# GpSimd's sums read their two operands 24 bytes apart modulo 32

## The chip, the core and the metric

The kernel runs on one core of one Trainium2 chip. A time is device microseconds of one execution, from the host's side of the device; the span is what the profiler shows between the first and the last instruction of one profiled execution. Every run computes the same layer stack on the same input.

## What is computed

Two layers of a decoder trunk on a sequence of 512 tokens and 1024 channels, in float32. Cut to what matters here:

```python
for l in range(DEPTH):                                   # DEPTH = 2
    x = x + 0.5 * swiglu(rms_norm(x, ffn1_norm[l]), gate1[l], up1[l], down1[l])   # D_FF = 2816
    h = rms_norm(x, mix_norm[l])
    a, g, q, k, v = split(h @ w_in[l])
    conv_out = silu(rms_norm(causal_depthwise_conv(a * sigmoid(g), conv_w[l]) + conv_b[l]))  # width 31
    diff_out = differential_attention(q, k, v, ...)
    x = x + concat([conv_out, diff_out]) @ w_out[l]
    x = x + 0.5 * swiglu(rms_norm(x, ffn2_norm[l]), gate2[l], up2[l], down2[l])
```

where `swiglu(h, g, u, d) = (silu(h @ g) * (h @ u)) @ d`. There are four feed-forward parts (two per layer) and two mixers.

## The kernel before

**Split weights.** A float32 matrix product is made of three products of rounded parts. Each weight tile arrives by DMA in a buffer `wraw` (128 partitions x 1024 columns, a ring of five). ScalarE rounds it into `whi` (L101, L364), VectorE or GpSimd subtracts the rounded part and writes the rest into `wlo` (L102, L368). TensorE then multiplies hi x hi, hi x lo and lo x hi. `chunk` loads such a tile for the plain products and the mixer; `by_halves` and `gather` are variants for single places.

**Units.** Each feed-forward part first does five blocks of hidden features in the plain way, and the other 17 in *units*. A unit makes a two by two block product from seven smaller ones instead of eight (Strassen's scheme in Winograd's form). For this it needs sums of weight blocks as well as the blocks: GpSimd makes them, four per unit, in `Unit.sums` (L355 to L358): `d` from a gate and an up block, `u1 + u2` in place, then `m0` and `m1`, each made from the one before. There are 17 gate and up units (`GateUp`) and 8 down units (`Down`) in each feed-forward part, 100 in all. One unit keeps TensorE busy for some 10 us. A unit's raw weights lie in three buffers of the `wraw` ring, called A (`u`), B (`g`) and C (`more`, for `m0` and `m1`), and one buffer of 512 columns, D (`d`), of which there is only one. So the first sum of a unit's load waits for VectorE's `lo("D")` of the unit before.

**Order.** `Unit.body` writes out the order of a unit: it loads the next unit, goes through its own seven products, and between them calls the next unit's `hi` and `lo` for A, B, D, C, and what is left of the previous ones (`rest`, `finish`, `combine`). A tile scheduler places the instructions on each engine; every engine then works strictly in its own order. ScalarE also moves finished products out of PSUM (`keep`, L396, L413, L433); the next product into that bank waits for it. `combine` (L685 to L692) makes sums of hidden features, `hold` and `hs`, which the down units read; after the last gate and up unit of a group it is called at once (`soon`).

**The mixer.** GpSimd makes all 31 taps of one of four channel groups of the convolution and 10 taps of another: ScalarE multiplies a shifted `u` by a tap (L971, `prod`), GpSimd adds it to `yp` (L972). Squares of the result are summed in `csum` (L953), and `conv_finish` multiplies the result by a row factor (L998) and subtracts rounded parts (L1003). The convolution's input tile `u` has PAD = 30 columns of zeros in front, so its data starts 120 bytes into the tile. VectorE makes the other taps (L986), reading the same `u` at every shift. All tiles of the mixer and the units start at multiples of 32 bytes in a partition. The part `wlo` of the chunks for queries, keys, values and the output projection is made by GpSimd (L102), raw minus hi.

**Space.** `ones_r` is made wider by `SPACE` unused columns, which sets where later tiles lie.

Of the kernel before, what the change touches and what calls it, by code (L numbers as in the profile page):

```python
# [11 lines left out]
F32 = mybir.dt.float32  # L12
F32R = mybir.dt.float32r
I32 = mybir.dt.int32
AF = mybir.ActivationFunctionType
ALU = mybir.AluOpType
AX = mybir.AxisListType

P = 128
DEPTH = 2  # L20
SEQ = 512
# [8 lines left out]
TAPS = 31  # L30
# [15 lines left out]
PLAIN = PARTS[0][1]  # L46
PIN = False

SPACE = 392

POOL_TAPS = (TAPS, 0, 0, 10)

# [16 lines left out]
def trunk(ctx: ExitStack, tc: tile.TileContext, xt, par, lamv, relb, onehot,  # L69
          gu1, dn1, wag, wqkv, wout, gu2, dn2, out):  # L70
    nc = tc.nc
    V, S, G, T = nc.vector, nc.scalar, nc.gpsimd, nc.tensor

    const = ctx.enter_context(tc.tile_pool(name="const", bufs=1))
    small = ctx.enter_context(tc.tile_pool(name="small", bufs=2))
    act = ctx.enter_context(tc.tile_pool(name="act", bufs=1))
    wp = ctx.enter_context(tc.tile_pool(name="wp", bufs=1))
    tmp = ctx.enter_context(tc.tile_pool(name="tmp", bufs=2))
# [3 lines left out]
    def f32(ap):  # L82
        return ap.bitcast(F32)
# [7 lines left out]
    RING = {"wraw": 5, "whi": 4, "wlo": 4, "wraw2": 1, "whi2": 2, "wlo2": 2}  # L91

    def ring(tag, n=1024):
        dt = F32 if "raw" in tag else F32R
        return wp.tile([P, n], dt, tag=tag, name=tag, bufs=RING[tag])

# [7 lines left out]
            tc.keep_in_program_order(low)  # L104

    def chunk(src, eng=None, pin=False):
        raw, hi, lo = ring("wraw"), ring("whi"), ring("wlo")
        nc.sync.dma_start(raw, src)
        parts_of(raw, hi, lo, eng, pin=pin)
        return hi, lo  # L110

    def by_halves(src):

        raw, got = ring("wraw"), []
        nc.sync.dma_start(raw, src)
        for h in (slice(0, 512), slice(512, 1024)):
            got.append((ring("whi2", 512), ring("wlo2", 512)))
            parts_of(raw[:, h], *got[-1])
        return got
# [35 lines left out]

    ones_r = const.tile([P, P + SPACE], F32R, tag="ones_r", name="ones_r")[:, :P]
    V.memset(f32(ones_r), 1.0)
# [8 lines left out]
    for k0, k1 in ((0, 1), (1, 4), (4, KT)):  # L166
        h = slice(k0 * P, k1 * P)
# [14 lines left out]
    def col(l, name, i=0):  # L182
        c = _AT[name] + i
        return pars[l][:, c : c + 1]
# [149 lines left out]
    def pinned(ins, pin=PIN):  # L334
        if pin:
            tc.keep_in_program_order(ins)
        return ins
# [4 lines left out]
    def by_two(t):  # L342
        return t.rearrange("p (n c) -> p n c", n=2)

    class Unit:
# [3 lines left out]

        def __init__(self, fp):  # L350
            self.fp = fp
            self.parts, self.raw, self.cols = {}, {}, {}

        def sums(self, u1, u2, g1, g2, d, m0, m1):
            G.tensor_tensor(d, g1, u1, op=ALU.add)  # L355
            G.tensor_tensor(u1, u1, u2, op=ALU.add)  # L356
            G.tensor_tensor(m0, u1, g1, op=ALU.add)  # L357
            G.tensor_tensor(m1, m0, g2, op=ALU.add)  # L358

        def hi(self, k, pin=PIN):  # L360
            tag, n = self.WIDE[k]
            hi, lo = ring("whi" + tag, n), ring("wlo" + tag, n)
            self.parts[k] = hi, lo
            pinned(S.activation(hi[:, : self.cols[k]], self.raw[k][:, : self.cols[k]], AF.Copy), pin)  # L364

        def lo(self, k, pin=PIN):
            (hi, lo), c = self.parts[k], self.cols[k]
            pinned(V.tensor_tensor(out=lo[:, :c], in0=self.raw[k][:, :c], in1=f32(hi[:, :c]), op=ALU.subtract), pin)  # L368

        def w(self, k, b):  # L370
            c = slice(b * P, (b + 1) * P)
# [83 lines left out]
    class GateUp(Unit):  # L455
# [5 lines left out]
            self.soon = n == 2 * gated.pairs - 1 and n + 1 == gated.many  # L461

        def load(self):
            u, g = ring("wraw"), ring("wraw")
            nc.sync.dma_start(u, self.src[1])
            nc.sync.dma_start(g, self.src[0])
            d, more = ring("wraw2", 512), ring("wraw")
            h = slice(0, 512), slice(512, 1024)
            self.sums(u[:, h[0]], u[:, h[1]], g[:, h[0]], g[:, h[1]], d, more[:, h[0]], more[:, h[1]])
            self.raw = {"A": u, "B": g, "C": more, "D": d}  # L470
            self.cols = {k: n for k, (_, n) in self.WIDE.items()}

        AT = {"u2u1": ("A", 0), "u2": ("A", 4), "g1": ("B", 0), "g2": ("B", 4), "g1u2u1": ("C", 0), "all": ("C", 4),
              "g1u1": ("D", 0)}
# [28 lines left out]
    class Down(Unit):  # L503
# [7 lines left out]
        def load(self):  # L511
            A, B = 2 * self.q, 2 * self.q + 1
            whole, over, J = min(self.many, 8), max(self.many - 8, 0), self.steps * P

            def pull(raw, at, m, k, end):
                while k < end:
                    half, f = divmod(self.m0 + k, HALF)
                    b, w = m * HALF + f, 1
                    while (b + w) % 8 and k + w < end and f + w < HALF:
                        w += 1  # L520
                    c = b % 8
                    nc.sync.dma_start(raw[:, at : at + w * P], self.dn[half, b // 8][:, c * P : (c + w) * P])
                    at, k = at + w * P, k + w

            u, g, d = ring("wraw"), ring("wraw"), ring("wraw2", 512)
            pull(u, 0, B, 0, whole)
            pull(g, 0, A, 0, whole)
            more = ring("wraw")
            at = {"D": J, "C": 2 * J}
            raw = {"D": d, "C": more}  # L530
            where = ("D", "D") if J + 2 * over * P <= 512 else ("D", "C")
            self.ninth = []
            for n, m in enumerate((A, B)):
                k = where[n]
                self.ninth.append((k, at[k] // P))
                pull(raw[k], at[k], m, whole, self.many)
                at[k] += over * P

            def odd_even(t):
                t = t[:, : 2 * J].rearrange("p (j e c) -> p e j c", e=2, c=P)  # L540
                return t[:, 0], t[:, 1]

            def row(t, n):
                return t[:, n * J : (n + 1) * J].rearrange("p (j c) -> p j c", c=P)

            self.sums(*odd_even(u), *odd_even(g), row(d, 0), row(more, 0), row(more, 1))
            self.raw = {"A": u, "B": g, "C": more, "D": d}
            self.cols = {"A": whole * P, "B": whole * P, **at}

        def weights(self, wt, j):  # L550
            k, b = {"u2u1": ("A", 2 * j), "u2": ("A", 2 * j + 1), "g1": ("B", 2 * j), "g2": ("B", 2 * j + 1),
# [287 lines left out]
    def mixer(l, pr, after, turn):  # L839
        with tc.tile_pool(name="mix", bufs=1) as mp, tc.tile_pool(name="mt", bufs=2) as mt:  # L840
# [104 lines left out]
            csum = mp.tile([P, SEQ], F32, tag="csum", name="csum")  # L945

            def conv_square(c, y):
                if c == 0:
                    S.activation(csum, y, AF.Square)
                else:  # L950
                    sq = mt.tile([P, SEQ], F32, tag="csq", name="csq", bufs=1)
                    S.activation(sq, y, AF.Square)
                    G.tensor_tensor(csum, csum, sq, op=ALU.add)  # L953

                if c == CT - 1:
                    for k in range(CT):
                        tc.keep_in_program_order(
                            G.tensor_scalar(ys[k], ys[k], ghalf[l][:, k : k + 1], None, op0=ALU.mult)
                        )

            def conv_taps(c, n, then=None):

                wc = _AT["conv_w"] + c * TAPS
                yp = None
                if n:
                    yp = mp.tile([P, SEQ], F32, tag="yp%d" % (n < TAPS), name="yp")
                    G.tensor_scalar(yp, us[c][:, 0:SEQ], pars[l][:, wc : wc + 1], col(l, "conv_b", c),
                                    op0=ALU.mult, op1=ALU.add)
                    for t in range(1, n):
                        p = mt.tile([P, SEQ], F32, tag="prod", name="prod")  # L970
                        S.activation(p, us[c][:, t : t + SEQ], AF.Copy, scale=pars[l][:, wc + t : wc + t + 1])  # L971
                        G.tensor_tensor(yp, yp, p, op=ALU.add)  # L972
                if n == TAPS:
                    ys[c] = yp
                    conv_square(c, yp)
                    return
                y = bank("y", "ps_y")
                if not n:
                    V.tensor_scalar(y, us[c][:, 0:SEQ], pars[l][:, wc : wc + 1], col(l, "conv_b", c),
                                    op0=ALU.mult, op1=ALU.add)  # L980
                else:
                    V.tensor_scalar(y, us[c][:, n : n + SEQ], pars[l][:, wc + n : wc + n + 1], None, op0=ALU.mult)

                ys[c] = us[c][:, PAD:]
                for t in range(n + 1 if n else 1, TAPS):
                    V.scalar_tensor_tensor(ys[c] if t == PAD and not n else y, us[c][:, t : t + SEQ],  # L986
                                           pars[l][:, wc + t : wc + t + 1], y, op0=ALU.mult, op1=ALU.add)
                if then is not None:
                    then()
                if n:  # L990
                    V.tensor_tensor(ys[c], y, yp, op=ALU.add)
                conv_square(c, ys[c])
# [137 lines left out]
            for half, t in ((0, slice(0, SEQ)), (1, slice(SEQ // 2, SEQ)), (1, slice(0, SEQ // 2))):  # L1130
                if t.stop == SEQ:
                    w = [None] * 4 if half else wo
                for m in range(KT):
# [3 lines left out]
                    for kk in range(4):  # L1137
                        k = half * 4 + kk
# [108 lines left out]
```

## Time and profile before

| | |
|---|---|
| median of 3 runs | 1775.47 us (1773.9 to 1775.86) |
| the profiled execution | 1775.77 us |
| its span | 1774.0 us |
| granted TensorE clock | 0.999 |
| TensorE busy | 99% of the span |
| VectorE, GpSimd, ScalarE busy | 80%, 56%, 56% |
| DMA | 177.89 MB, mean 100 GB/s |

Busy shares say which engine is full over the whole span; TensorE is. A row of a group gives the line, the engine, output and inputs, the count, then the busy time in us and the mean duration in ns, then the engine's idle time ahead of those instructions and what ended it. A row of the waits reads: who waited, for whom, us in total, times, the longest. A row of the timeline or of the chain starts with the start in us from the span's beginning and the duration in us. Durations of TensorE's matmuls overlap, so its pace is read from the distance of starts.

### The profile page before, as it was taken

The page shows a single profiled execution, that of the slowest core. Times are in us where ns is not written, and L with a number is a line of the kernel's source. Part 1 is how long each engine was busy: PE and PEld are TensorE (multiplying, and loading weights), DVE is VectorE, ACT ScalarE, POOL GpSimd, SP SyncE. Part 2 cuts the span into 40 slices and gives each one's busy share as a digit, 9 for nine tenths or more (in the row PEclk, how much of TensorE's full clock was granted, in tenths as well). Part 3 has the DMA queues.
Part 4 walks back from the last instruction along what each step waited for, and adds up shares of the span by engine and source line. Part 5 has one row for each costly group of instructions (what it writes and reads, how often), then busy time and mean ns, then how long its engine had stood idle before and what let it go on. Part 6 is the DMA issues. An engine that isn't in the chain of part 4 may idle for free.

```text
span 1774.0 us, 30565 instructions
## 1 busy us (share of the span) xinstructions
PE 1762.0 (99%) x11869; PEld 1624.0 (92%) x11869; DVE 1418.2 (80%) x2021; ACT 996.4 (56%) x1591; POOL 999.9 (56%) x665
## 2 busy tenths in 40 slices
PE   9999999999999999999999999999999999999999
PEld 7899999988788899999988999999887888999998
DVE  6978878868857978888778788887788588788785
ACT  6456566545844456556534665665558354565663
POOL 3176666369863156766403666653798532567661
PEclk9999999999999999999999999999999999999999
DMA  6232333332122223323332333324231232333332
GB/s 225 91 117 98 108 108 105 124 106 96 36 84 84 84 96 108 108 96 114 112 108 71 103 101 108 108 94 157 71 110 34 72 108 71 108 96 108 108 105 75
DMA packets 74226, 177.89 MB, mean 100 GB/s; under 512 B 8951, under 2 KB 30726, under 8 KB 74080
## 3 DMA queue, kind: packets, MB, share of 16 engines
q1 hardware_dynamic: 72480, 174.10, 29.9%
q8 instruction: 93, 1.52, 0.4%
q0 software_dynamic: 1312, 1.67, 0.3%
q14 instruction: 53, 0.43, 0.1%
q10 hardware_dynamic: 288, 0.16, 0.0%
HBM read 173.79 MB, written 3.42 MB: 100 GB/s over the span
## 4 chain that ended last, share of the span: by engine, by line
PE 84%; DVE 9%; issue 3%; POOL 2%; ACT 1%; DMA 1%; SPq 0%; DVEq 0%; ACTq 0%
PE ps_pair L378 44%; PE ps_pair L142 5%; PE ps_pair L141 5%; PE ps_pair L138 5%; DVE wlo L368 4%; PE ps_d L141 2%; PE ps_d L138 2%; PE ps_d L142 2%; PE ps_sc L1018 2%; PE ps_d L378 2%; PE ps_pair L894 2%; PE ps_pair L896 2%; PE ps_pair L895 2%; PE ps_out L138 1%; PE ps_out L142 1%
## 5 line engine op out<-in xcount | busy, mean ns | idle before, releaser
L368 DVE TENSOR_TENSOR wlo<-wraw,whi 128x1024 fp32r<-128x1024 f32 (+2 forms) x400 | 527.1, 1318 | 152.6 <-ACT whi L364 152.0
L364 ACT ACTIVATE whi<-wraw 128x1024 fp32r<-128x1024 f32 (+2 forms) x400 | 378.1, 948 | 312.1 <-PE ps_pair L378 135.7
L355 POOL TENSOR_TENSOR wraw<-wraw 128x512 f32<-128x512 f32 (+1 forms) x100 | 132.2, 1322 | 518.4 <-DVE wlo L368 315.3
L378 PE MATMUL ps_pair<-acth,wlo 128*128 128x256 f32 x1088 | 307.9, 283 | 0.0
L378 PE MATMUL ps_pair<-actl,whi 128*128 128x256 f32 x1088 | 307.9, 283 | 0.0
L378 PE MATMUL ps_pair<-acth,whi 128*128 128x256 f32 x1088 | 307.9, 283 | 0.0
L378 PE MATMUL ps_pair<-th,whi 128*128 128x256 f32 x816 | 232.1, 284 | 0.8
L378 PE MATMUL ps_pair<-tl,whi 128*128 128x256 f32 x816 | 230.9, 283 | 0.0
L378 PE MATMUL ps_pair<-th,wlo 128*128 128x256 f32 x816 | 230.8, 283 | 0.0
L378 PEld LDWEIGHTS ps_pair<-actl,whi 128*128 128x128 f32 x1088 | 208.9, 192 | 0.2
L378 PEld LDWEIGHTS ps_pair<-acth,whi 128*128 128x128 f32 x1088 | 208.9, 192 | 0.2
L378 PEld LDWEIGHTS ps_pair<-acth,wlo 128*128 128x128 f32 x1088 | 208.9, 192 | 0.0
L101 ACT ACTIVATE whi<-wraw 128x1024 fp32r<-128x1024 f32 (+3 forms) x124 | 122.9, 1001 | 148.9 <-PE ps_pair L141 84.7
L358 POOL TENSOR_TENSOR wraw<-wraw 128x512 f32<-128x512 f32 (+1 forms) x100 | 179.7, 1797 | 7.8
L141 PE MATMUL ps_pair<-actl,whi 128*128 128x512 f32 x448 | 174.8, 391 | 0.3 <-DVE actl L227 0.2
L138 PE MATMUL ps_pair<-acth,whi 128*128 128x512 f32 x448 | 173.9, 393 | 0.6 <-ACT whi L101 0.6
L142 PE MATMUL ps_pair<-acth,wlo 128*128 128x512 f32 x448 | 174.1, 391 | 0.0
L357 POOL TENSOR_TENSOR wraw<-wraw 128x512 f32<-128x512 f32 (+1 forms) x100 | 167.9, 1679 | 7.8
L356 POOL TENSOR_TENSOR wraw<-wraw 128x512 f32<-128x512 f32 (+1 forms) x100 | 166.5, 1665 | 7.6
L378 PEld LDWEIGHTS ps_pair<-th,whi 128*128 128x128 f32 x816 | 156.5, 192 | 2.8 <-ACT keep L433 2.4
L378 PEld LDWEIGHTS ps_pair<-tl,whi 128*128 128x128 f32 x816 | 156.6, 192 | 0.0
L378 PEld LDWEIGHTS ps_pair<-th,wlo 128*128 128x128 f32 x816 | 156.6, 192 | 0.0
(205 smaller groups left out, 4458.6 us busy)
## 6 DMA issues: line engine op xcount, KB each, us to landing
wraw<-in_gu SPq DMA_DIRECT2D x172, 512.0 KB, 3.5
wraw<-in_wqkv SPq DMA_DIRECT2D x24, 512.0 KB, 3.5
wraw<-in_wag SPq DMA_DIRECT2D x16, 512.0 KB, 3.5
wraw<-in_wout SPq DMA_DIRECT2D x16, 512.0 KB, 3.5
wraw<-in_dn SPq DMA_DIRECT2D x60, 128.0 KB, 2.9
wraw<-in_dn SPq DMA_DIRECT2D x20, 384.0 KB, 3.2
wraw<-in_dn SPq DMA_DIRECT2D x28, 256.0 KB, 2.9
wraw<-in_dn SPq DMA_DIRECT2D x20, 320.0 KB, 3.1
```

The lines of the kernel that those rows point to most:

```text
L101: S.activation(hi, raw, AF.Copy)
L138: first = T.matmul(ps, wh, xh, start=start, stop=False)
L141: T.matmul(ps, wh, xl, start=False, stop=False)
L142: T.matmul(ps, wl, xh, start=False, stop=stop)
L355: G.tensor_tensor(d, g1, u1, op=ALU.add)
L356: G.tensor_tensor(u1, u1, u2, op=ALU.add)
L357: G.tensor_tensor(m0, u1, g1, op=ALU.add)
L358: G.tensor_tensor(m1, m0, g2, op=ALU.add)
L364: pinned(S.activation(hi[:, : self.cols[k]], self.raw[k][:, : self.cols[k]], AF.Copy), pin)
L368: pinned(V.tensor_tensor(out=lo[:, :c], in0=self.raw[k][:, :c], in1=f32(hi[:, :c]), op=ALU.subtract), pin)
L378: mm = T.matmul(ps, l, r, start=first and i == n == 0, stop=False, skip_group_check=True)
L894: T.matmul(ps[n], xh[:, t], wh, start=k == 0, stop=False)
```

## The change

GpSimd's two-operand sums get operands whose start addresses differ by 24 bytes modulo 32, where the layout allows it. `GAP` is 6 columns, 24 bytes. The tiles `wraw` become 1040 columns wide and get a pool of their own; `chunk` and a unit's `g` use the 1024 columns behind the gap. In a gate and up unit, `u` is a view of two halves of 512 columns with 6 unused columns behind each, so `u1` starts at 0 and `u2` at 2072 bytes, 24 modulo 32; its DMA writes two runs of 2 KB into each partition instead of one of 4 KB. In a down unit `u` stays at 0, and its two operands alternate inside one tile, 512 bytes apart. The sums' targets `d` and `more` stay at 0. `yp` and `csq` are set off by the gap in wider tiles. In the sums the operand at 24 is named first. `SPACE` shrinks from 392 to 312 columns; `x`, `acth`, `actl` and `rb` lie 20480 bytes higher, since `wraw` now lies ahead of them, `whi` and the tiles of the units where they were, and those of the mixer behind `yp` 64 to 96 bytes higher. On every engine the instructions stand in the same order as before, and DMAs too.

```diff
-SPACE = 392
+SPACE = 312
+GAP = 6
+WRAW = 1040
...
+    rp = ctx.enter_context(tc.tile_pool(name="rp", bufs=1))
...
     def ring(tag, n=1024):
+        if tag == "wraw":
+            return rp.tile([P, WRAW], F32, tag=tag, name=tag, bufs=RING[tag])
...
     def chunk(src, eng=None, pin=False):
-        raw, hi, lo = ring("wraw"), ring("whi"), ring("wlo")
+        raw, hi, lo = ring("wraw")[:, GAP : GAP + 1024], ring("whi"), ring("wlo")
...
         def sums(self, u1, u2, g1, g2, d, m0, m1):
             G.tensor_tensor(d, g1, u1, op=ALU.add)
-            G.tensor_tensor(u1, u1, u2, op=ALU.add)
-            G.tensor_tensor(m0, u1, g1, op=ALU.add)
-            G.tensor_tensor(m1, m0, g2, op=ALU.add)
+            G.tensor_tensor(u1, u2, u1, op=ALU.add)
+            G.tensor_tensor(m0, g1, u1, op=ALU.add)
+            G.tensor_tensor(m1, g2, m0, op=ALU.add)
...
         def load(self):                                   # GateUp
-            u, g = ring("wraw"), ring("wraw")
-            nc.sync.dma_start(u, self.src[1])
+            u = by_two(ring("wraw")[:, : 1024 + 2 * GAP])[:, :, :512]
+            g = ring("wraw")[:, GAP : GAP + 1024]
+            nc.sync.dma_start(u, by_two(self.src[1]))
             nc.sync.dma_start(g, self.src[0])
-            d, more = ring("wraw2", 512), ring("wraw")
+            d, more = ring("wraw2", 512), ring("wraw")[:, :1024]
             h = slice(0, 512), slice(512, 1024)
-            self.sums(u[:, h[0]], u[:, h[1]], g[:, h[0]], g[:, h[1]], d, more[:, h[0]], more[:, h[1]])
+            self.sums(u[:, 0], u[:, 1], g[:, h[0]], g[:, h[1]], d, more[:, h[0]], more[:, h[1]])
...
-            u, g, d = ring("wraw"), ring("wraw"), ring("wraw2", 512)      # Down.load
+            u, g = ring("wraw")[:, :1024], ring("wraw")[:, GAP : GAP + 1024]
+            d = ring("wraw2", 512)
...
-                    sq = mt.tile([P, SEQ], F32, tag="csq", name="csq", bufs=1)
+                    sq = mt.tile([P, SEQ + 8], F32, tag="csq", name="csq", bufs=1)[:, GAP : GAP + SEQ]
                     S.activation(sq, y, AF.Square)
-                    G.tensor_tensor(csum, csum, sq, op=ALU.add)
+                    G.tensor_tensor(csum, sq, csum, op=ALU.add)
...
-                    yp = mp.tile([P, SEQ], F32, tag="yp%d" % (n < TAPS), name="yp")
+                    yp = mp.tile([P, SEQ + 8], F32, tag="yp%d" % (n < TAPS), name="yp")[:, GAP : GAP + SEQ]
```

`Unit.hi` and `Unit.lo` take the shape of their tiles from the raw view (a new helper `like`) instead of a count of columns.

More of the change, by code (lines that the diff above doesn't have):

```diff
@@ L112, in by_halves @@
     def by_halves(src):
-        raw, got = ring("wraw"), []
+        raw, got = ring("wraw")[:, :1024], []
         nc.sync.dma_start(raw, src)
@@ L351, in __init__ @@
             self.fp = fp
-            self.parts, self.raw, self.cols = {}, {}, {}
+            self.parts, self.raw = {}, {}
         def sums(self, u1, u2, g1, g2, d, m0, m1):
             G.tensor_tensor(d, g1, u1, op=ALU.add)
-            G.tensor_tensor(u1, u1, u2, op=ALU.add)
-            G.tensor_tensor(m0, u1, g1, op=ALU.add)
-            G.tensor_tensor(m1, m0, g2, op=ALU.add)
+            G.tensor_tensor(u1, u2, u1, op=ALU.add)
+            G.tensor_tensor(m0, g1, u1, op=ALU.add)
+            G.tensor_tensor(m1, g2, m0, op=ALU.add)
         def hi(self, k, pin=PIN):
@@ L363, in hi, with like @@
             self.parts[k] = hi, lo
-            pinned(S.activation(hi[:, : self.cols[k]], self.raw[k][:, : self.cols[k]], AF.Copy), pin)
+            raw, hi = self.raw[k], self.like(k, hi)
+            pinned(S.activation(hi, raw, AF.Copy), pin)
         def lo(self, k, pin=PIN):
-            (hi, lo), c = self.parts[k], self.cols[k]
-            pinned(V.tensor_tensor(out=lo[:, :c], in0=self.raw[k][:, :c], in1=f32(hi[:, :c]), op=ALU.subtract), pin)
+            raw, hi, lo = self.raw[k], *(self.like(k, t) for t in self.parts[k])
+            pinned(V.tensor_tensor(out=lo, in0=raw, in1=f32(hi), op=ALU.subtract), pin)
+        def like(self, k, t):
+            return by_two(t) if len(self.raw[k].shape) == 3 else t[:, : self.raw[k].shape[1]]
         def w(self, k, b):
@@ L463, in load @@
         def load(self):
-            u, g = ring("wraw"), ring("wraw")
-            nc.sync.dma_start(u, self.src[1])
+            u = by_two(ring("wraw")[:, : 1024 + 2 * GAP])[:, :, :512]
+            g = ring("wraw")[:, GAP : GAP + 1024]
+            nc.sync.dma_start(u, by_two(self.src[1]))
             nc.sync.dma_start(g, self.src[0])
-            d, more = ring("wraw2", 512), ring("wraw")
+            d, more = ring("wraw2", 512), ring("wraw")[:, :1024]
             h = slice(0, 512), slice(512, 1024)
-            self.sums(u[:, h[0]], u[:, h[1]], g[:, h[0]], g[:, h[1]], d, more[:, h[0]], more[:, h[1]])
+            self.sums(u[:, 0], u[:, 1], g[:, h[0]], g[:, h[1]], d, more[:, h[0]], more[:, h[1]])
             self.raw = {"A": u, "B": g, "C": more, "D": d}
-            self.cols = {k: n for k, (_, n) in self.WIDE.items()}
         AT = {"u2u1": ("A", 0), "u2": ("A", 4), "g1": ("B", 0), "g2": ("B", 4), "g1u2u1": ("C", 0), "all": ("C", 4),
@@ L523, in pull @@
                     at, k = at + w * P, k + w
-            u, g, d = ring("wraw"), ring("wraw"), ring("wraw2", 512)
+            u, g = ring("wraw")[:, :1024], ring("wraw")[:, GAP : GAP + 1024]
+            d = ring("wraw2", 512)
             pull(u, 0, B, 0, whole)
             pull(g, 0, A, 0, whole)
-            more = ring("wraw")
+            more = ring("wraw")[:, :1024]
             at = {"D": J, "C": 2 * J}
@@ L546, in load @@
             self.sums(*odd_even(u), *odd_even(g), row(d, 0), row(more, 0), row(more, 1))
-            self.raw = {"A": u, "B": g, "C": more, "D": d}
-            self.cols = {"A": whole * P, "B": whole * P, **at}
+            cols = {"A": whole * P, "B": whole * P, **at}
+            self.raw = {k: t[:, : cols[k]] for k, t in (("A", u), ("B", g), ("C", more), ("D", d))}
         def weights(self, wt, j):
```

## The prediction

> **What bounds the kernel now.** I read the page's first part, then the waits of TensorE's weight loads, then the chain of waits and the timelines around the longest of those waits, and last the groups of GpSimd instructions. A change of 0.2% (3.6 us) is about what a measurement of this kernel can tell from no change.
>
> ```profile
> span 1774.0 us, 30565 instructions
> PE 1762.0 (99%) x11869; PEld 1624.0 (92%) x11869; DVE 1418.2 (80%) x2021; ACT 996.4 (56%) x1591; POOL 999.9 (56%) x665
> PEld ps_pair L378 <- DVE hs L691: 2.5, 4, 0.6
> PEld ps_pair L378 <- ACT keep L433: 2.4, 8, 0.3
> ```
>
> TensorE is busy for 99% of the span, so GpSimd's 999.9 us are not the time. What a faster GpSimd can give back is what TensorE waits for because of it. In the feed-forward units the weight loads waited twelve times: four times for VectorE's hs (2.5 us), eight times for ScalarE's keep (2.4 us). A wait costs a little more than itself:
>
> ```profile
> 132.57 0.28 PE L378 MATMUL ps_pair<-tl,whi 128*128 128x256 f32 x1
> 132.69 0.28 PE L378 MATMUL ps_pair<-th,wlo 128*128 128x256 f32 x1
> 133.08 0.39 PE L378 MATMUL ps_pair<-th,whi 128*128 128x256 f32 x1
> 133.30 0.28 PE L378 MATMUL ps_pair<-tl,whi 128*128 128x256 f32 x1
> ```
>
> In an undisturbed stretch such matmuls start every 0.12 us (132.57, 132.69). The next start, at 133.08, comes 0.39 after that, which is 0.27 lost, and the one behind it another 0.22 later: 0.10 more than the pace. Twelve waits and twelve such restarts are 4.9 + 12 x 0.10 = 6.1 us. That is the most which the feed-forward parts can return.
>
> Behind the keep waits stands GpSimd. The chain of waits at the first of them:
>
> ```profile
> 127.47 0.60 DVE wlo L368
> ...
> 128.13 1.30 POOL wraw L355
> 129.44 0.07 issue
> 129.51 2.17 POOL wraw L356
> ...
> 131.70 0.03 ACT whi L364
> ...
> 132.66 0.37 ACT keep L433
> ...
> 133.08 0.98 PE ps_pair L378 x6
> ```
>
> ```profile
> 129.04 1.47 DVE L368 TENSOR_TENSOR wlo<-wraw,whi 128x1024 fp32r<-128x1024 f32 x1
> 184.78 1.21 DVE L368 TENSOR_TENSOR wlo<-wraw,whi 128x1024 fp32r<-128x1024 f32 x1
> ```
>
> VectorE's part of D frees the one D buffer, GpSimd makes d (L355) and then the sum in A (L356), ScalarE rounds A, and only behind that, in its order, stands the keep for which TensorE waits. L356 took 2.17 us here, L355 1.30. The reason lies in VectorE: its wlo came up at 129.04 while L355 ran, took 1.47 us where an undisturbed one takes 1.21, and L356 ended 1.15 us after wlo did. Each of the two waits out the other when both read two operands in SBUF. [...]
>
> Behind the hs waits stands the same exclusion, three times in a row on VectorE:
>
> ```profile
> 179.34 1.29 POOL L356 TENSOR_TENSOR wraw<-wraw 128x512 f32<-128x512 f32 x1
> 180.71 1.36 POOL L357 TENSOR_TENSOR wraw<-wraw 128x512 f32<-128x512 f32 x1
> 182.15 2.16 POOL L358 TENSOR_TENSOR wraw<-wraw 128x512 f32<-128x512 f32 x1
> 179.45 1.47 DVE L686 SCALAR_TENSOR_TENSOR hold<-hold 128x256 f32<-128x256 f32 x1
> 180.84 2.32 DVE L368 TENSOR_TENSOR wlo<-wraw,whi 128x1024 fp32r<-128x1024 f32 x1
> 183.41 1.45 DVE L692 TENSOR_TENSOR hs<-hold,hs 128x512 fp32r<-128x512 f32 x1
> 186.51 0.41 DVE L691 TENSOR_TENSOR hs<-ps_pair,hs 128x256 fp32r<-128x256 f32 x1
> 186.98 0.39 PE L378 MATMUL ps_pair<-hs,whi 128*128 128x256 f32 x1 [0.44 <-DVE hs L691]
> ```
>
> **What one sum will take.** The program's order stays as it is on every engine; only addresses change, and which operand of a sum is named first. The trace of before has both kinds of address:
>
> ```profile
> L355 POOL TENSOR_TENSOR wraw<-wraw 128x384 f32<-128x384 f32 x16 | 16.3, 1019 | 74.8 <-DVE wlo L368 65.0 <-DMA wraw<-in_dn 9.9
> L972 POOL TENSOR_TENSOR yp<-yp,prod 128x512 f32<-128x512 f32 x78 | 101.1, 1297 | 10.0 <-ACT prod L971 7.4
> L102 POOL TENSOR_TENSOR wlo<-wraw,whi 128x1024 fp32r<-128x1024 f32 x44 | 105.5, 2403 | 31.7 <-ACT whi L101 31.7
> L998 POOL TENSOR_TENSOR u<-u,rb 128x512 f32<-128x512 f32 x6 | 6.4, 1098 | 0.0
> L998 POOL TENSOR_TENSOR yp<-yp,rb 128x512 f32<-128x512 f32 x2 | 2.5, 1273 | 2.0 <-ACT rb L213 2.0
> L1003 POOL TENSOR_TENSOR actl<-u,acth 128x512 fp32r<-128x512 f32 x6 | 6.6, 1094 | 2.9 <-ACT acth L1002 2.8
> ```
>
> At L998 the channels in u start PAD = 30 columns into their tile, 120 bytes, which is 24 modulo 32; the other operand starts at a multiple of 32, and so do both operands of the yp form. The same line takes 1098 ns with the 24 and 1273 without; L1003 with it takes 1094, and two operands at 0 take 1297 in L972. A sum of 512 columns therefore falls from 1.29 to 1.10 us, 0.19 less, and I take this for every changed operation; for 384 columns I scale it to 0.14 and for L102's 1024 to 0.39 (estimates). [...]
>
> The units' sums are 84 groups of 512 and 16 of 384 columns; d, m0 and m1 change in all of them, u1 + u2 in the 68 gate and up units alone, since in a down unit both operands of L356 lie in one tile. That is (3 x 84 + 68) x 0.19 + 48 x 0.14 = 67.5 us. With L102 (44 x 0.39 = 17.2), L972 (78 x 0.19 = 14.8) and the csum and yp steps (about 1.8), GpSimd loses some 101 us of its 999.9. Nearly all of it lies beside TensorE's work and is worth nothing.
>
> **What of it is on the path.** At 128 us, in a gate and up load: L355 ends 0.19 earlier, the wlo that waits for it too, L356 another 0.19 earlier: ScalarE's rounding and keep come 0.38 sooner. TensorE lost 0.27 and a restart of 0.10, so this wait goes. At the hs wait, a down load, L355 gives 0.19, L686 then ends 0.19 sooner, L357 0.38, the wlo behind it 0.38, L358 0.57, and hs L692, which waited for L358, 0.57; hs L691 follows directly. The wait was 0.73 - 0.12 = 0.61 by the matmul's start, so it shrinks to about 0.05 and sometimes vanishes. What is late next is TensorE itself. Over the twelve places I count 6.1 us less 4 x 0.1 us for remainders and restarts: 5.7 us.
>
> **Costs of the new addresses.** VectorE and ScalarE now read raw weights at 24:
>
> ```profile
> L986 DVE SCALAR_TENSOR_TENSOR ps_y<-u,par,ps_y x156: 739/756/758, 378.3 to 1346.9; 128x512 f32<-128x512 f32 x156
> L971 ACT ACTIVATE prod<-u,par x78: 702/712/728, 369.9 to 1353.4; 128x512 f32<-128x512 f32 x78
> ```
>
> Both lines read u from every multiple of 4 bytes, and their extremes lie 3 and 4% apart; I take nothing. A VectorE operation with one SBUF operand at 24 and one at 0 isn't in the trace; 3% either way would move a wlo of 1.21 us by 0.04, a fifth of what one sum saves. The loads of gates, mixer chunks and downs' g now land at 24, and those of up weights in two pieces of 2 KB per partition:
>
> ```profile
> POOL wraw L355 <- DVE wlo L368: 315.3, 87, 9.5
> POOL wraw L355 <- DMA wraw<-in_gu: 156.2, 8, 35.8
> wraw<-in_gu SPq DMA_DIRECT2D x172, 512.0 KB, 3.5
> bias<-d SPq DMA_DIRECT2D x2, 1024.0 KB, 6.0
> 120.47 0.33 SPq L466 DMA_DIRECT2D wraw<-in_gu  x1
> q1 hardware_dynamic: 72480, 174.10, 29.9%
> ```
>
> No row shows a write off a multiple of 32. The nearest is bias, read from rows 2556 bytes apart: 6.0 us for 1 MB against 3.5 for half, so reading off the boundary is not dear. A gate load issued at 120.47 lands near 124.0 and is first read at 128.13: 4.1 us to spare, and 87 of the 100 units waited last for VectorE's part of D, 8 for a load. A landing later by up to 4 us is covered in such a unit; beyond that each microsecond would be paid in each of some 68 units. [...] I take 0 and keep the loss for the rivals.
>
> The profiled execution took 1775.77 us around its span of 1774.0, 0.30 above the median 1775.47. Less 5.7 it gives 1770.1; against the median, 1769.8.
>
> **Rivals.**
> 1. *The small saving* (8%). [...] If nothing at all changes (6%), 1775.5.
> 2. *The order of the exclusion turns* (14%), the slower side. GpSimd now comes up 0.2 to 0.6 us sooner, and where VectorE got in first it may find GpSimd there. L686 paid 1.47 - 0.48 = 1.0 us for that. In the stretch behind the last gate and up unit hs is urgent, at two places per feed-forward part: eight places x 1.0 = 8 us more, less the 3.2 that the keep waits return: 1780. It decides where a GpSimd start and a VectorE start now lie within 0.2 us of each other. For it: 179.34 and 179.45. Against it: there VectorE is already the one that waits, and it waits less.
> 3. *The loads are late* (8%). Landing after 8 us in place of 3.5, past the 4.1 us to spare, would cost 0.4 us in each of 68 units, 27 us less 5.7: 1797. Against it: the transfers take 29.9% of the engines' time.
>
> **How the numbers follow.** The forecast has 64%: 1769.8, and from 1768.2 (all twelve waits, with an attention wait or two) to 1771.5 (the hs waits half left). All of it lies under 1771.9, faster by over 0.2%. Rival 1 in both forms (14%) and a mild half of rival 2 (5%), where it merely eats the gain, are within 0.2%. The rest of rival 2 (9%) and rival 3 (8%) are slower. Left out at the top are these 17%, so the range ends at 1777.0. Faster 0.64, same 0.19, slower 0.17.
>
> **What would show it.** Right: L355, L357, L358 and L972 near 1.10 us where nothing is in their way, L356 at 1.10 in gate and up loads and 1.29 in down loads, POOL's busy time near 900 us, both waits of the weight loads at L378 nearly gone. Wrong in the price: L972 still at 1.29. Wrong in the path: sums at 1.10 and the keep or hs waits still there. Wrong in the cover: waits of L355 for loads in more than a dozen units, or landings well over 3.5 us.

## Result and the profile after

| | before | after |
|---|---|---|
| median | 1774.51 us (6 runs, 1773.47 to 1775.86) | 1767.89 us (6 runs, 1767.6 to 1769.68) |
| ratio, 95% interval | | 0.9965 [0.9952, 0.9977] |
| span of the profiled execution | 1774.0 us | 1765.8 us |
| granted TensorE clock | 0.999 | 1.0 |

The change makes the kernel 0.35% faster, 6.2 us by the ratio (4.1 to 8.5 by its interval). The forecast was 1769.8 us, 1.9 above the median: 1.0 of that lies in before, whose median was 1775.47 us when the forecast was made and is 1774.51 here, and 0.9 in the change itself (6.6 us by the two medians, where 5.7 were forecast).

The first part of the page after and its chain of waits by engine. Behind the change every line is 5 to 10 higher: the sums are L360 to L363, the units' `wlo` L374, their `whi` L370, their matmuls L387, the keep L442, the steps of hold and hs L695 to L702, `yp` L982, `csum` L963 and the mixer's `wlo` L107.

```profile
span 1765.8 us, 30565 instructions
PE 1756.3 (99%) x11869; PEld 1620.8 (92%) x11869; DVE 1394.2 (79%) x2021; ACT 989.1 (56%) x1591; POOL 869.5 (49%) x665
PE 97%; DVE 2%; DMA 0%; issue 0%; SPq 0%; ACT 0%; DVEq 0%
```

GpSimd lost 130.4 us of its 999.9. In the chain of waits of before TensorE had 84%, the rest lay on the other engines; now the chain is TensorE's for 97%. Of the weight loads, these two groups of before hold the twelve waits (the last column is idle time ahead, and what ended it):

```profile
L378 PEld LDWEIGHTS ps_pair<-th,whi 128*128 128x128 f32 x816 | 156.5, 192 | 2.8 <-ACT keep L433 2.4
L378 PEld LDWEIGHTS ps_pair<-hs,whi 128*128 128x128 f32 x672 | 105.9, 192 | 3.5 <-DVE hs L691 2.5
```

The same groups after:

```profile
L387 PEld LDWEIGHTS ps_pair<-th,whi 128*128 128x128 f32 x816 | 156.7, 192 | 0.0
L387 PEld LDWEIGHTS ps_pair<-hs,whi 128*128 128x128 f32 x672 | 105.7, 192 | 1.0
```

All twelve are gone, keep and hs alike. By the distances of TensorE's starts the units lost 6.3 us in before and nothing in after. The two spans differ by 8.2 us: before's execution also lost some 0.4 us at the start and 1.5 us in the first layer's attention, where TensorE's granted clock was 0.51 from 494.9 to 498.4 us (1.00 there in after). `e1_gap8` below has the waits of before and loses neither (clock 1.0, span 1772.1 us), and of the six executions of after the two at a clock of 0.999 took 1769.27 and 1769.68 us, the four at 1.0 took 1767.6 to 1767.91. So both belong to the single execution and not to the change.

The groups of GpSimd after, operand forms apart (busy us, mean ns, then idle time ahead):

```profile
L362 POOL TENSOR_TENSOR wraw<-wraw 128x512 f32<-128x512 f32 x84 | 157.5, 1875 | 6.6
L363 POOL TENSOR_TENSOR wraw<-wraw 128x512 f32<-128x512 f32 x84 | 125.0, 1488 | 6.6
L361 POOL TENSOR_TENSOR wraw<-wraw 128x512 f32<-128x512 f32 x84 | 101.5, 1208 | 6.6
L107 POOL TENSOR_TENSOR wlo<-wraw,whi 128x1024 fp32r<-128x1024 f32 x44 | 87.9, 2001 | 45.6 <-ACT whi L106 45.4
L982 POOL TENSOR_TENSOR yp<-yp,prod 128x512 f32<-128x512 f32 x78 | 85.2, 1093 | 24.5 <-ACT prod L981 22.1
```

L982 is the clean reading: 1297 to 1093 ns. L107 fell by 402 ns (390 were reckoned). The means of the unit sums hold the exclusion as well, and it has moved. In before:

```profile
L358 POOL TENSOR_TENSOR wraw<-wraw 128x512 f32<-128x512 f32 x84 | 158.0, 1881 | 6.6
L356 POOL TENSOR_TENSOR wraw<-wraw 128x512 f32<-128x512 f32 x84 | 147.2, 1753 | 6.6
L357 POOL TENSOR_TENSOR wraw<-wraw 128x512 f32<-128x512 f32 x84 | 146.0, 1738 | 6.6
```

The second sum (L356, now L361) fell by 545 ns, far over 190, and the third (L357, now L362) rose by 137. The timeline after at the first keep place (where the first wait for keep stood) shows why:

```profile
126.38 1.09 POOL L360 TENSOR_TENSOR wraw<-wraw 128x512 f32<-128x512 f32 x1 [5.09 <-DVE wlo L374]
127.56 1.09 POOL L361 TENSOR_TENSOR wraw<-wraw 128x512 f32<-128x512 f32 x1
128.72 1.96 POOL L362 TENSOR_TENSOR wraw<-wraw 128x512 f32<-128x512 f32 x1
127.79 1.93 DVE L374 TENSOR_TENSOR wlo<-wraw,whi 128x1024 fp32r<-128x1024 f32 x1 [0.41 <-ACT whi L370]
126.70 1.06 ACT L370 ACTIVATE whi<-wraw 128x1024 fp32r<-128x1024 f32 x1 [0.78 <-PE ps_pair L387]
129.56 1.06 ACT L370 ACTIVATE whi<-wraw 128x1024 fp32r<-128x1024 f32 x1 [1.32 <-POOL wraw L361]
130.53 0.36 ACT L442 ACTIVATE keep<-ps_pair 128x256 f32<-128x256 f32 x1
```

In before VectorE's `wlo` of C of the load ahead (in `Unit.body` C follows D, whose `lo` frees the first sum) came up while the first sum ran, and the second sum waited it out. Now the first sum starts so early that the second is already running when that `wlo` comes up at 127.79; it is held behind the second sum (1.93 in place of 1.21 us), and the third sum behind it (1.96 in place of 1.30). With an operand in PSUM there is no such hold in before's trace: L485, whose first operand is `ps_pair`, takes 680 to 694 ns at all its 68 places, 29 of them wholly inside a fourth sum (L358). `wlo` of 1024 columns (L368), with both operands in SBUF, takes 1.47 us in the median when it starts beside a GpSimd sum and 1.22 with none beside it. `wlo` can't come sooner, since ScalarE's rounding of that C (126.70) waits for TensorE. All eight keep places show this order. The second sum ends at 128.65, 0.9 us ahead of the rounding at 129.56: the row names L361 as its releaser, but that was long done.

At the first hs place, after, against the rows of 179.34 to 186.51 in the prediction:

```profile
177.22 1.30 POOL L361 TENSOR_TENSOR wraw<-wraw 128x512 f32<-128x512 f32 x1
178.60 1.16 POOL L362 TENSOR_TENSOR wraw<-wraw 128x512 f32<-128x512 f32 x1
179.84 1.95 POOL L363 TENSOR_TENSOR wraw<-wraw 128x512 f32<-128x512 f32 x1
177.54 1.26 DVE L696 SCALAR_TENSOR_TENSOR hold<-hold 128x256 f32<-128x256 f32 x1
178.72 2.12 DVE L374 TENSOR_TENSOR wlo<-wraw,whi 128x1024 fp32r<-128x1024 f32 x1
181.10 1.24 DVE L702 TENSOR_TENSOR hs<-hold,hs 128x512 fp32r<-128x512 f32 x1
184.00 0.41 DVE L701 TENSOR_TENSOR hs<-ps_pair,hs 128x256 fp32r<-128x256 f32 x1
```

The order of the exclusion is that of before, at all four hs places, and each link is 0.2 shorter. The second sum of a down load, both of whose operands lie in one tile, is still 1.30; `hold` (L696) waits less beside it only because it comes up later in it (0.32 us behind its start, 0.11 in before).

### The profile page after: what moved, and what is told of

Its sections match the earlier page's. It is cut to its first block, busy times and chain, and to the rows that moved or that the text cites. A ratio compares the mean times of both kernels' runs of the same rounds, so it can differ in the third digit from the quotient of the medians.

```text
span 1765.8 us, 30565 instructions
## 1 busy us (share of the span) xinstructions
PE 1756.3 (99%) x11869; PEld 1620.8 (92%) x11869; DVE 1394.2 (79%) x2021; ACT 989.1 (56%) x1591; POOL 869.5 (49%) x665
## 4 chain that ended last, share of the span: by engine, by line
PE 97%; DVE 2%; DMA 0%; issue 0%; SPq 0%; ACT 0%; DVEq 0%
PE ps_pair L387 57%; PE ps_pair L147 5%; PE ps_pair L146 5%; PE ps_pair L143 5%; PE ps_d L147 2%; PE ps_d L146 2%; PE ps_d L143 2%; PE ps_sc L1028 2%; PE ps_d L387 2%; PE ps_pair L904 2%; PE ps_pair L905 2%; PE ps_pair L906 2%; PE ps_out L146 1%; PE ps_out L147 1%; PE ps_out L143 1%; PE ps_o L1058 1%
## 5 line engine op out<-in xcount | busy, mean ns | idle before, releaser
L374 DVE TENSOR_TENSOR wlo<-wraw,whi 128x1024 fp32r<-128x1024 f32 (+2 forms) x400 | 505.6, 1264 | 167.3 <-ACT whi L370 166.6
L370 ACT ACTIVATE whi<-wraw 128x1024 fp32r<-128x1024 f32 (+2 forms) x400 | 379.2, 949 | 329.4 <-PE ps_pair L387 184.5
L360 POOL TENSOR_TENSOR wraw<-wraw 128x512 f32<-128x512 f32 (+1 forms) x100 | 113.1, 1131 | 605.9 <-DVE wlo L374 393.9
L387 PE MATMUL ps_pair<-acth,wlo 128*128 128x256 f32 x1088 | 307.9, 283 | 0.0
L387 PE MATMUL ps_pair<-actl,whi 128*128 128x256 f32 x1088 | 307.9, 283 | 0.0
L387 PE MATMUL ps_pair<-acth,whi 128*128 128x256 f32 x1088 | 307.9, 283 | 0.0
L387 PE MATMUL ps_pair<-th,whi 128*128 128x256 f32 x816 | 230.9, 283 | 0.0
L387 PE MATMUL ps_pair<-tl,whi 128*128 128x256 f32 x816 | 230.9, 283 | 0.0
L387 PE MATMUL ps_pair<-th,wlo 128*128 128x256 f32 x816 | 230.9, 283 | 0.0
L387 PEld LDWEIGHTS ps_pair<-actl,whi 128*128 128x128 f32 x1088 | 208.9, 192 | 0.2
L387 PEld LDWEIGHTS ps_pair<-acth,whi 128*128 128x128 f32 x1088 | 208.9, 192 | 0.2
L106 ACT ACTIVATE whi<-wraw 128x1024 fp32r<-128x1024 f32 (+3 forms) x124 | 123.2, 1002 | 153.0 <-PE ps_pair L146 85.7
L387 PEld LDWEIGHTS ps_pair<-acth,wlo 128*128 128x128 f32 x1088 | 208.9, 192 | 0.0
L362 POOL TENSOR_TENSOR wraw<-wraw 128x512 f32<-128x512 f32 (+1 forms) x100 | 176.5, 1765 | 7.8
L387 PEld LDWEIGHTS ps_pair<-th,whi 128*128 128x128 f32 x816 | 156.7, 192 | 0.0
L387 PEld LDWEIGHTS ps_pair<-tl,whi 128*128 128x128 f32 x816 | 156.7, 192 | 0.0
L387 PEld LDWEIGHTS ps_pair<-th,wlo 128*128 128x128 f32 x816 | 156.7, 192 | 0.0
L363 POOL TENSOR_TENSOR wraw<-wraw 128x512 f32<-128x512 f32 (+1 forms) x100 | 143.1, 1431 | 7.8
L387 PE MATMUL ps_pair<-hl,whi 128*128 128x256 f32 (+1 forms) x496 | 145.6, 294 | 0.0
```

Source lines behind the costliest of these rows:

```text
L106: S.activation(hi, raw, AF.Copy)
L362: G.tensor_tensor(m0, g1, u1, op=ALU.add)
L363: G.tensor_tensor(m1, g2, m0, op=ALU.add)
L370: pinned(S.activation(hi, raw, AF.Copy), pin)
L374: pinned(V.tensor_tensor(out=lo, in0=raw, in1=f32(hi), op=ALU.subtract), pin)
L387: mm = T.matmul(ps, l, r, start=first and i == n == 0, stop=False, skip_group_check=True)
```

## The experiments

The theory: a sum at a distance of 24 bytes is 0.19 us shorter, and that alone, in the units, takes the twelve waits away. Against it stand: the new layout does it (tiles and pools moved, loads split in two); the mixer's sums do it; the addresses ease the exclusion itself rather than the duration.

**`e1_gap8`: the same layout and split, a distance of 32 bytes.**

```diff
-GAP = 6
+GAP = 8
```

> The changed kernel with a gap of 8 columns (32 bytes) in place of 6 (24 bytes): the same pools, tile sizes, loads in two pieces and order of operands, only the distance of the two operands is 0 modulo 32 again. Theory (the sums' own duration): sums of 512 columns at 1.29 us again, GpSimd busy about 1000 us, all twelve waits of the weight loads at the units' products back (about 4.9 us in all), time 1774.5, ratio to before 1.000. Rival (layout: x, acth, actl lying 20480 bytes higher, the ring in a pool of its own): as the changed kernel, 1768, ratio 0.9965.

Measured: 1773.91 us, ratio 0.9999 [0.999, 1.0008]. Its waits of the weight loads:

```profile
PEld ps_pair L387 <- ACT keep L442: 2.6, 8, 0.3
PEld ps_pair L387 <- DVE hs L701: 2.6, 4, 0.7
```

Everything is back: the waits, sums of 1.29, GpSimd at 1000.8 us. The layout, the order of the operands and the split load are worth nothing that can be measured.

**`e2_units` and `e3_rest`: the units alone, and all but the units.** In e2:

```diff
-        raw, hi, lo = ring("wraw")[:, GAP : GAP + 1024], ring("whi"), ring("wlo")
+        raw, hi, lo = ring("wraw")[:, :1024], ring("whi"), ring("wlo")
...
-                    sq = mt.tile([P, SEQ + 8], F32, tag="csq", name="csq", bufs=1)[:, GAP : GAP + SEQ]
+                    sq = mt.tile([P, SEQ + 8], F32, tag="csq", name="csq", bufs=1)[:, :SEQ]
...
-                    yp = mp.tile([P, SEQ + 8], F32, tag="yp%d" % (n < TAPS), name="yp")[:, GAP : GAP + SEQ]
+                    yp = mp.tile([P, SEQ + 8], F32, tag="yp%d" % (n < TAPS), name="yp")[:, :SEQ]
```

> The gap of 24 bytes in the units alone; the mixer's chunks, yp and csq start at 0. Theory: all of the gain lies in the units, no waits at the units' products, ratio 0.9965, 1768.3; GpSimd busy some 33 us more than in the changed kernel, about 903 us. Rival (the mixer's 33 us of GpSimd time carry a part): ratio 0.998 or more.

Measured: 1768.03 us, ratio 0.9964 [0.9952, 0.9977], none of the twelve waits, GpSimd 903.1 us. In e3:

```diff
-            u = by_two(ring("wraw")[:, : 1024 + 2 * GAP])[:, :, :512]
-            g = ring("wraw")[:, GAP : GAP + 1024]
+            u = by_two(ring("wraw")[:, : 1024 + 2 * 8])[:, :, :512]
+            g = ring("wraw")[:, 8 : 8 + 1024]
...
-            u, g = ring("wraw")[:, :1024], ring("wraw")[:, GAP : GAP + 1024]
+            u, g = ring("wraw")[:, :1024], ring("wraw")[:, 8 : 8 + 1024]
```

> The gap of 24 bytes in the mixer's chunks, yp and csq alone; in the units the gap is 32 bytes, so their sums read at 0 modulo 32. Theory: the twelve waits are all there, ratio 1.000, 1774.5. Rival (mixer): ratio under 0.999.

Measured: 1774.26 us, ratio 1.0 [0.9991, 1.0009], GpSimd 965.8 us, both waits at 2.6 us. So 35.0 us less work for GpSimd (1000.8 - 965.8) buys nothing beside the mixer's TensorE work, and the units' share buys all of it.

**`e4_short`: addresses as before, one sum shorter.** In the kernel of before the second sum covers 21 of 32 columns:

```diff
-            G.tensor_tensor(u1, u1, u2, op=ALU.add)
+            part = (slice(None),) * (len(u1.shape) - 1) + (slice(0, u1.shape[-1] * 21 // 32),)
+            G.tensor_tensor(u1[part], u1[part], u2[part], op=ALU.add)
```

> The kernel before, with all addresses as they were, but the units' second sum (u1 + u2) made over 21 of each 32 columns only (336 of 512); the rest of A keeps u1, which leaves out that part of the computation. By its duration (0.19 fixed and 2.17 ns a column) it takes 0.91 us in place of 1.29. Theory (a shorter sum is enough, whatever the addresses): the eight waits for keep vanish, the four for hs shrink from 0.61 to about 0.25 us each; ratio 0.9975, 1770.0. Rival (the addresses do it in another way: ScalarE or VectorE reading the raw weights, or other tiles): ratio 1.000 with the waits in place.

Measured: 1768.46 us, ratio 0.9966 [0.9954, 0.9979]. Its second sum and the two groups of weight loads:

```profile
L357 POOL TENSOR_TENSOR wraw<-wraw 128x336 f32<-128x336 f32 x84 | 103.1, 1228 | 6.6
L379 PEld LDWEIGHTS ps_pair<-th,whi 128*128 128x128 f32 x816 | 156.7, 192 | 0.0
L379 PEld LDWEIGHTS ps_pair<-hs,whi 128*128 128x128 f32 x672 | 105.7, 192 | 1.0
```

A sum made shorter by other means gives the same gain at the old addresses, so a shorter duration on the path is enough, and the gain needs nothing else that the addresses might do. They don't ease the exclusion either: in after `wlo` and the third sum still wait each other out (1.93 and 1.96 above). The expectation still missed: hs waits were to be left, and none was. Shortening one of four sums took more than was reckoned for it. The 0.19 fixed and 2.17 ns a column in the expectation are an estimate from two rows of before, 1297 ns for 512 columns (L972) and 1019 for 384 (L355).

**`e5_distance`: the disputed price by itself.** Chains of four equal GpSimd adds, nothing beside them, one line for each distance of the first operand from the second; then VectorE subtracts and loads of 512 KB at several starts.

```diff
...
+    [keep(add(o[:, 0:512], a[:, 2:514], b[:, 0:512], op=ALU.add)) for _ in range(4)]   # 8 bytes
...
+    [keep(add(o[:, 0:512], a[:, 6:518], b[:, 6:518], op=ALU.add)) for _ in range(4)]   # both at 24
...
```

> A kernel that leaves out the whole computation and measures single operations by themselves: GpSimd adds of 512 columns with the first operand 0, 4, 8, 12, 16, 20, 24, 28, 32, 40, 48 and 56 bytes behind the second (both tiles start at a multiple of 64 bytes), the second 8, 16, 24 and 56 bytes behind the first, both at 24, the distance of 24 made with 32 and 8 and with 56 and 32, and the output at 24; VectorE subtractions of 1024 columns at 0, 8, 16, 24, 32 and 56 bytes and with the second operand at 24; loads of 512 KB that land at 0, 8, 16, 24, 32, 56 and 64 bytes and in two pieces of 2 KB, one after the other. Theory (the distance modulo 32 counts): 1.29 us at 0 and 32, 1.10 at 24 and 56 and with 32 and 8, 1.29 with both at 24; the second operand at 8 behind the first is the distance -8, also 1.10; other distances between. VectorE: 1.21 at all distances. Loads: 3.5 us everywhere. Rival (a start off the boundary counts, not the distance): 1.10 with both at 24 too. Rival (the distance counts modulo 64, as at the lines seen before, -8): 1.10 at 56 and less gain at 24. Rival (writes off the boundary are dear): landings at 8 to 56 bytes well over those at 0, 32 and 64.

The groups of this kernel. L41 to L49 are distances of 0, 4, 8 and so on to 32 bytes; in L59 both operands start at 24; in L60 the first starts at 32 and the second at 8; L67 and L70 are VectorE at distances 0 and 24:

```profile
L41 POOL TENSOR_TENSOR o<-a,b 128x512 f32<-128x512 f32 x4 | 5.1, 1265 | 2.5 <-DVE o L36 2.2
L42 POOL TENSOR_TENSOR o<-a,b 128x512 f32<-128x512 f32 x4 | 5.0, 1257 | 0.3
L43 POOL TENSOR_TENSOR o<-a,b 128x512 f32<-128x512 f32 x4 | 4.4, 1089 | 0.3
L44 POOL TENSOR_TENSOR o<-a,b 128x512 f32<-128x512 f32 x4 | 4.4, 1088 | 0.3
L45 POOL TENSOR_TENSOR o<-a,b 128x512 f32<-128x512 f32 x4 | 5.0, 1262 | 0.3
L46 POOL TENSOR_TENSOR o<-a,b 128x512 f32<-128x512 f32 x4 | 5.0, 1258 | 0.3
L47 POOL TENSOR_TENSOR o<-a,b 128x512 f32<-128x512 f32 x4 | 4.4, 1088 | 0.3
L48 POOL TENSOR_TENSOR o<-a,b 128x512 f32<-128x512 f32 x4 | 4.4, 1094 | 0.3
L49 POOL TENSOR_TENSOR o<-a,b 128x512 f32<-128x512 f32 x4 | 5.0, 1262 | 0.3
L59 POOL TENSOR_TENSOR o<-a,b 128x512 f32<-128x512 f32 x4 | 5.1, 1263 | 0.3
L60 POOL TENSOR_TENSOR o<-a,b 128x512 f32<-128x512 f32 x4 | 4.4, 1088 | 0.3
L67 DVE TENSOR_TENSOR vo<-va,vb 128x1024 f32<-128x1024 f32 x4 | 4.9, 1225 | 0.1
L70 DVE TENSOR_TENSOR vo<-va,vb 128x1024 f32<-128x1024 f32 x4 | 4.9, 1225 | 0.1
```

The distance decides, not the start (1263 ns in L59, 1088 in L60), and it counts modulo 16 bytes: 0 and 4 are slow (1257 to 1265 ns), 8 and 12 fast (1088 to 1094). The further lines agree: 40 and 56 bytes 1089 and 1088 ns, 48 bytes 1262, and with the second operand ahead by 8, 24 and 56 fast (1088 to 1092), by 16 slow (1262). VectorE pays nothing at any of the distances tried (1225 to 1226 ns).

The loads, from issue to landing, of this kernel at 24 bytes (L83) and in two pieces of 2 KB (L86):

```profile
DMA to landing us min/median/max: 3.1/3.3/3.4
DMA to landing us min/median/max: 3.5/3.7/3.8
```

At starts of 0, 8, 16, 32, 56 and 64 bytes the median was 3.3 to 3.4 as well. A start off the boundary costs nothing at the starts tried; the second piece costs 0.4 us (3.7 against 3.3).

**`e6_gap2` and `e7_gap4`: 8 and 16 bytes in the kernel itself.** `GAP = 2` and `GAP = 4` in place of 6.

> The changed kernel with a gap of 2 columns (8 bytes). From the single measurements (fast at distances of 8, 12, 24, 28, 40 and 56 bytes, slow at 0, 4, 16, 20, 32 and 48: a period of 16 bytes). Theory: sums of 512 columns at 1.10 us, no waits at the units' products, ratio 0.9965, 1768. Rival (only 24 modulo 32 helps): sums at 1.29, ratio 1.000.

> The changed kernel with a gap of 4 columns (16 bytes): half of the way to 32, off the 32-byte boundary as 8 and 24 are. Theory (period of 16 bytes): sums at 1.29 us, all twelve waits back, ratio 1.000, 1774.5. Rival (any distance other than 0 modulo 32): ratio 0.9965.

Measured: 8 bytes 1768.42 us, ratio 0.9963 [0.995, 0.9976], none of the waits, GpSimd 870.6 us; 16 bytes 1775.68 us, ratio 1.0002 [0.9993, 1.0012], both waits at 2.6 us, GpSimd 1000.5 us. The period of 16 holds in the kernel as well.

**`e8_u2`, `e9_g`, `e10_down`: which sums.** Outside the units the 24 bytes stay. Of the units' sums, e8 leaves only the second of gate and up loads short (both `g` at 32 bytes). e9 makes that one long again and leaves the others short (8 unused columns behind each half of `u`, so its halves start 2080 bytes apart, 0 modulo 32). e10 leaves only the down loads' sums short.

```diff
 e8, GateUp, and for g in the same way in Down:
-            g = ring("wraw")[:, GAP : GAP + 1024]
+            g = ring("wraw")[:, 8 : 8 + 1024]
 e9, GateUp:
-            u = by_two(ring("wraw")[:, : 1024 + 2 * GAP])[:, :, :512]
+            u = by_two(ring("wraw")[:, : 1024 + 2 * 8])[:, :, :512]
 e10, GateUp: both of these lines with 8 in place of GAP
```

> The gap of 24 bytes in u (its second half) and outside the units, but g at 32 bytes: of a gate and up unit's four sums the second alone is short, of a down unit's none. Theory: L355's successor starts as before, so the second sum ends 0.19 us sooner in gate and up loads: the keep waits at those shrink from 0.3 to about 0.1 us each, the four hs waits, in down loads, stay at 0.6; waits in all about 3.2 us in place of 4.9, ratio 0.999, 1773. Rival (every 0.19 us counts alike): half of the gain, 0.998.

> The reverse: g at 24 bytes, u's second half at a distance of 0 modulo 32 (a gap of 16 columns between the halves' ends and starts): first, third and fourth sum short in all units, the second in none. [...] Rival (the second sum's own 0.19 is needed): some keep waits of about 0.1 us remain, ratio 0.9975.

> The gap of 24 bytes in g of the down units and outside the units; in gate and up units both gaps are 32 bytes. Short are the first, third and fourth sum of 32 down loads, none of the 68 gate and up loads. The prediction's steps (each wait by the savings of its own load): the four hs waits go (0.57 of 0.61 us, with their restarts 2.8 us in all), the four small keep waits in down loads go (0.7 in all), the eight large keep waits in gate and up loads stay (2.9): ratio 0.998, 1771.5. Rival (the hs waits live on VectorE's delay from the gate and up loads ahead): some 0.3 us of each hs wait stays, ratio 0.9988.

Measured: e8 1768.92 us, ratio 0.9968 [0.9956, 0.9979]; e9 1769.25 us, 0.9968 [0.9956, 0.998]; e10 1771.91 us, 0.9984 [0.9975, 0.9994]. The wait that is left in e10:

```profile
PEld ps_pair L387 <- ACT keep L442: 2.6, 8, 0.3
```

e10 came as the steps of the prediction have it: the down loads' sums take the hs waits, and the keep waits stay whole. Its ratio alone can't tell 0.998 from the rival's 0.9988; its waits do, since no hs wait is left in them. In e9 the rival didn't come: no keep or hs wait is left, though the second sum takes 1.29 us again. The order of the exclusion is turned as in after: at the first keep place the second sum starts at 127.40 and `wlo` of C at 127.44, which takes 2.33 us. Its units lose nothing, as after; its profiled execution, at a clock of 0.999, has a span of 1766.9 us. e8 is a miss: it was to shrink the keep waits alone, and the hs waits nearly went as well.

**`e11_u2_again`: e8 once more,** to see what is left and whether it repeats.

> The kernel with a short second sum in gate and up loads alone, once more for its waits, since in the profile before TensorE's granted clock was 0.998. If the slower clock hid the hs waits, they are back at 0.3 us or more each and the ratio is 0.998; if the gate and up loads ahead shorten them, they are 0.1 us or less and the ratio 0.9968.

Measured: 1769.01 us, ratio 0.9969 [0.9957, 0.9981]. It repeats: by TensorE's starts 1.0 us is left in the units, mostly 0.08 and a restart of 0.10 at each of the four hs places. The cause can be read when each kernel's first places are set against TensorE's own progress there, so that losses ahead of the place drop out. Worked out from the traces, in us behind the start of one and the same matmul of the units' line: for the first three columns its 289th matmul, some 7 us ahead of the first keep place (at 125.61 in before and 125.12 in after), for the last two its 713th, some 10 us ahead of the first hs place (177.01 and 176.00):

| | first sum starts | second ends | keep starts | first sum, down load | hs (L701) starts |
|---|---|---|---|---|---|
| before | 2.53 | 6.05 | 7.06 | 0.95 | 9.50 |
| e1_gap8 | 2.52 | 6.04 | 7.04 | 0.93 | 9.49 |
| e10_down | 2.52 | 6.04 | 7.04 | 0.77 | 8.72 |
| e8_u2 | 2.13 | 5.45 | 6.46 | 0.41 | 8.97 |
| e4_short | 1.75 | 4.89 | 5.90 | 0.05 | 8.22 |
| e9_g | 1.46 | 3.92 | 5.42 | 0.05 | 8.01 |
| after | 1.27 | 3.53 | 5.42 | 0.05 | 8.00 |

TensorE lost 0.27 at the keep of 7.06 and 0.61 at the hs of 9.50, so it needs keep by 6.79 and hs by 8.89. A kernel whose keep starts under 6.79 has no wait there, and e8's hs is 0.08 late, which is what it still loses. A first sum starts when VectorE has freed D, and VectorE's delay comes from the loads ahead: shorter gate and up sums let the down load ahead of hs start 0.54 us sooner (0.95 to 0.41), and hs 0.53 sooner, without one down sum being shorter. Two parts are therefore not additive: e8 takes 5.3 of the 6.3 us, e10 3.2, both together 6.3.

## Why the prediction held, step by step

- **The price of a sum**: 0.19 us expected, 0.20 measured in the kernel (L982) and 0.18 alone (1265 to 1089). The kernel's own two sizes put it on the columns: before, 1297 ns for 512 (L972) and 1019 for 384 (L355) give 2.17 ns per column behind a fixed 186; after, 1093 for 512 and 866 for 384 (L360) give 1.77 behind a fixed 185. Less the 186, the 1088 of e5 leave 1.76 ns per column and its 1265 leave 2.11. These are estimates from the groups' means.
- **GpSimd's busy time**: about 900 us expected, 869.5 measured. The means of L361 to L363 carry 67.2 us of savings where 44.8 were reckoned: less waiting in the exclusion, on top of shorter sums.
- **The keep waits**: they went, as forecast, but the size of the step was wrong. Keep was to come 0.38 us sooner; by the table it came 1.64 sooner. The first sum starts 1.26 sooner, not at the same time, and the second no longer waits for `wlo`. At 5.42 keep no longer hangs on the sums: it starts there in after and in e9, though the second sum ends at 3.53 and at 3.92. So the surplus buys nothing.
- **The hs waits**: 0.57 of 0.61 sooner expected, 1.50 measured. Down loads alone give 0.78 (e10), 0.18 of it by an earlier first sum; what the gate and up loads ahead hand on was left out. So nothing remains at the four places, where the prediction kept 0.4 us.
- **The sum**: 5.7 us of at most 6.1. The units' loss was 6.3, all of it came back, and the measured ratio is 6.2 us. The forecast's row of all twelve waits (1768.2) was the case that came. The path was right, but its steps were sized far too small; that the total still came close is owed to the cap, which is what TensorE lost. That the cap itself fits is in part luck: 0.7 of the 6.3 us lay at four smaller keep places (0.07 and a restart of 0.10 each, the first at 173.6 us), which the prediction's twelve leave out.
- **VectorE and ScalarE at 24**: nothing expected; VectorE is 1225 ns at every distance in e5, and ScalarE's rounding of 1024 columns outside the units, mostly chunks, which lie at 24, takes 1058 ns after (L106) and 1057 before (L101).
- **Rival 1**, a small saving or no effect: it fell on the price (L982, 204 ns less); no run shows a small saving. The modulus is neither 32 nor 64 but 16 (e5: 1088 ns at 24 and 56 bytes, 1262 at 16 and 48).
- **Rival 2**, the order of the exclusion turns: it turned, at the keep places, but in GpSimd's favour where GpSimd was the urgent one. VectorE's `wlo` of C, which now waits, isn't urgent: no wait of TensorE came of it. At the hs places, where a turn would have cost, the order stayed.
- **Rival 3**, late loads: the landings of the up weights and of the gate weights, first in before (L465, L466), then after, in two pieces (L475) and at 24 (L476):

```profile
DMA to landing us min/median/max: 3.3/3.5/12.4
DMA to landing us min/median/max: 3.3/3.5/8.3
DMA to landing us min/median/max: 3.7/4.0/13.3
DMA to landing us min/median/max: 3.4/3.5/8.5
```

The first sum's waits for loads, after (us in total, times, longest):

```profile
POOL wraw L360 <- DMA wraw<-in_gu: 166.6, 10, 35.9
```

The 24 bytes cost nothing, the split 0.5 us, which the 4.1 us to spare cover: 10 units waited last for a load, 8 before. In e1, whose up weights are split in the same way, the median is also 4.0.

## What to carry to other kernels

Where an engine off the bound stands ahead of a wait of the bound, find the few places where it does and the slack that is missing there (here 0.27 and 0.61 us); all work saved elsewhere on it, here 35 us in the mixer, was worth nothing. In a chain that hands its delay from one load to the next, count the saving of each load ahead as well, and place events against the bound engine's own progress. Before laying operands out for a distance, time the operation at several: the smallest gap that works (8 bytes here, 1768.42 us) is enough.

## What was not expected of the hardware

A GpSimd sum of two float32 operands takes 1088 to 1094 ns for 512 columns when the starts differ by 8 or 12 bytes modulo 16, and 1257 to 1265 at 0 or 4. The three lines ahead of the prediction, at 24 against 0, could not tell 16 from 32. Why distances of 0 and 4 differ from 8 and 12 isn't shown by any run here. A load of 512 KB in two pieces per partition lands 0.4 to 0.5 us later than in one (3.7 against 3.3 us in e5, 4.0 against 3.5 in the kernel), and its start off the boundary doesn't matter at the starts tried (3.3 to 3.4 us).
